# Routing tail of a hybrid layer: tiles 4 and 5 sorted as a pair, router work per column half

## Chip, cores and metric

The kernel runs on one core of a Trainium2 chip. The metric is the device time of one execution in microseconds (us). The engines are TensorE (PE; its weight loads PEld), VectorE (DVE), ScalarE (ACT), GpSimd (POOL) and the SyncE queue (SP), which only issues transfers. Each engine executes its instructions in the order in which they are written for it, and waits on semaphores for the others.

## Reference

A layer on 1024 latent tokens of width 1024 with 256 context tokens. Attention and a gated scan (DeltaNet) run side by side on one input projection; an output projection and a gated residual join them. A router then lets each of 16 experts choose its 128 strongest tokens.

```python
x = x + g1 * y_lat
h2 = modulate(rmsnorm(x, norm2_w[l]), sh2, sc2)
x = x + g2 * expert_choice_ffn(h2, router_w[l], w_gate[l], w_up[l], w_down[l])

# expert_choice_ffn
affinity = jax.nn.softmax((h @ router_w).astype(jnp.float32), axis=-1)
gates, idx = lax.top_k(jnp.swapaxes(affinity, 1, 2), cap)      # cap = 128
xg = jax.vmap(lambda hb, ib: hb[ib])(h, idx)
hid = jax.nn.silu(jnp.einsum('becd,edf->becf', xg, w_gate)) * jnp.einsum('becd,edf->becf', xg, w_up)
y = jnp.einsum('becf,efd->becd', hid, w_down) * gates[..., None].astype(h.dtype)
```

## The kernel before

Stages in order of time: adaLN vectors and the input projection (to about 411 us); the rest of the scan together with attention (to about 876 us, TensorE the busy engine); the output stage per token tile of 128 (eight tiles, tile 7 ends at about 957 us); the routing tail (to about 986 us); 16 experts (to the end).

The output stage has three functions per tile `t`. `out_norm(t)` normalizes the scan's output and builds the two operands `mh` and `ml`. `out_mm(t)` multiplies them with the output weights in two halves of 512 columns, 24 matmuls into `ps_d` each (lines 1283 to 1285), and VectorE adds the residual per half (`xres<-ps_d,xres`, line 1286). `out_route(t)` transposes the tile (line 1301), copies the transposes to `xT`, multiplies with the router weights `rwm` (line 1306, two groups of four), takes the sum of squares (`j<-xres`, line 1312), forms `logit`, its maximum `mx` and the softmax `aff`, and writes the normalized row `xn` for the later gather.

The top 128 of 1024 tokens per expert are found by sorting. `top_in(t)` brings the probabilities of a segment of tiles (dictionary `SEG`: tiles 0 to 3 as one, then each tile alone) on partitions, `top_out(t)` sorts lists with 8-wide maxima (`srt`, `at`), moves the sorted lists to the 16 experts' partitions by selection matmuls, and merges. For tiles 0 to 3 the selection matmuls are `ps_t<-srt` (line 1411) and ScalarE copies them to `lists` (lines 1416 and 1417); VectorE merges them as `m_3x`, `m_3y`. For a single tile four lists of 32 go through `ps_l` (line 1403) and `lists` (VectorE, line 1405) and are joined as `j2` and `j1`. Each result is merged into the running top list, named `t4` to `t7`; one merge step is a max and a min instruction of VectorE (`bitonic`, lines 1347 and 1348), 14 for a merge of 128. The last is `t7x`; `m` is its smallest value, the threshold of each expert, and `route()` makes slots, indices (`idx`) and gathers (`xg<-h,idx`) from it. Then the first expert matmul can start (`ps_m<-ehi,xx`, line 1612).

The order on each engine is set by a list scheduler from the program's order, priorities and modelled times. `tc.high_priority(-LP)` around a `top_out` puts its instructions behind others that are ready; the selection matmuls of single tiles are raised with `HP`.

`router_consts` (line 1182) makes the router's constants from the adaLN vectors in memory (`modrow`): column loads into `m2c`, `sh2` and `A2`, the modulated router weights `rwm`, and the bias `rbias` by a product with ones (`ps_d<-rwbs`, line 1207). In the prelude of attention (about 411 to 426 us) TensorE also transposes k (`ps_a<-consts,ksplit`, line 1057, 40 matmuls) and q (`ps_t<-consts,sr_sp`, line 1081), and VectorE finishes the last gate rows `zz` (line 626) and casts `kts` (line 1061).

## Time and profile before

| | |
|---|---|
| time, median of 3 runs | 1571.92 us (1571.24 to 1575.38) |
| profiled execution, its time | 1576.82 us |
| profiled execution, its span | 1575.1 us |
| TensorE busy | 1453.7 us (92%) |
| VectorE busy | 1175.2 us (75%) |
| ScalarE busy | 941.5 us (60%) |
| GpSimd busy | 252.2 us (16%) |
| chain that ended last, by engine | PE 63%, DVE 16%, DMA 10%, ACT 5% |

The span is the time from the first to the last recorded instruction of the profiled execution; what lies around it is 1.7 us. Rows of the trace give the start of an instruction, its duration, engine, line, output and inputs with shapes, and in brackets the idle time of its engine just before it with what ended it. Rows with xN put N adjacent instructions together. A view of stretches gives busy time of every engine, the granted TensorE clock as a share of full speed and the busy share of the transfer engines.

### The profile page before, as it was taken

The page shows a single profiled execution, that of the slowest core. Times are in us where ns is not written, and L with a number is a line of the kernel's source. Part 1 is how long each engine was busy: PE and PEld are TensorE (multiplying, and loading weights), DVE is VectorE, ACT ScalarE, POOL GpSimd, SP SyncE. Part 2 cuts the span into 40 slices and gives each one's busy share as a digit, 9 for nine tenths or more (in the row PEclk, how much of TensorE's full clock was granted, in tenths as well). Part 3 has the DMA queues.
Part 4 walks back from the last instruction along what each step waited for, and adds up shares of the span by engine and source line. Part 5 has one row for each costly group of instructions (what it writes and reads, how often), then busy time and mean ns, then how long its engine had stood idle before and what let it go on. Part 6 is the DMA issues. An engine that isn't in the chain of part 4 may idle for free.

```text
span 1575.1 us, 25623 instructions
## 1 busy us (share of the span) xinstructions
PE 1453.7 (92%) x9416; PEld 1177.5 (75%) x9416; DVE 1175.2 (75%) x2456; ACT 941.5 (60%) x1513; POOL 252.2 (16%) x230
## 2 busy tenths in 40 slices
PE   4999998987899998999899994999999999999996
PEld 1887787887778777887677663888888887777775
DVE  1824578698677686466666588899999998988886
ACT  1815454434376543556756442788887877777763
POOL 0000003323111112101400112011111211341001
PEclk7899999998999999899999997999999999999999
DMA  9356825777835456532333655889999999999991
GB/s 336 115 185 207 289 77 176 216 242 252 216 86 165 125 166 190 150 98 68 125 110 121 220 215 220 338 323 405 392 389 399 392 379 337 383 353 357 377 359 29
DMA packets 187049, 377.28 MB, mean 240 GB/s; under 512 B 47631, under 2 KB 124187, under 8 KB 159403
## 3 DMA queue, kind: packets, MB, share of 16 engines
q1 hardware_dynamic: 176320, 339.94, 61.3%
q0 software_dynamic: 7488, 29.36, 6.3%
q10 hardware_dynamic: 3115, 6.34, 1.0%
q8 instruction: 74, 1.21, 0.3%
q14 instruction: 52, 0.43, 0.1%
HBM read 321.91 MB, written 53.68 MB: 238 GB/s over the span
## 4 chain that ended last, share of the span: by engine, by line
PE 63%; DVE 16%; DMA 10%; ACT 5%; issue 3%; POOL 1%; SPq 1%; POOLq 0%; ACTq 0%; DVEq 0%
PE ps_m L1617 9%; PE ps_m L1612 8%; PE ps_m L1614 8%; PE ps_t L1130 4%; DVE elo L1599 4%; PE ps_a L1113 3%; PE ps_t L1123 3%; PE ps_s L442 3%; PE ps_s L444 3%; PE ps_s L443 3%; PE ps_d L976 1%; DMA woraw<-in_w_out 1%; PE ps_d L297 1%; PE ps_d L982 1%; PE ps_d L991 1%
## 5 line engine op out<-in xcount | busy, mean ns | idle before, releaser
L1599 DVE TENSOR_TENSOR elo<-eraw,ehi 128x2048 fp32r<-128x2048 f32 x102 | 229.2, 2285 | 16.1 <-ACT ehi L1588 16.0
L1588 ACT ACTIVATE ehi<-eraw 128x2048 fp32r<-128x2048 f32 x105 | 199.3, 1926 | 43.2 <-PE ps_m L1614 38.2
L1612 PE MATMUL ps_m<-ehi,xx 128*128 128x512 f32 x512 | 161.7, 397 | 2.2 <-ACT ehi L1588 2.2
L1614 PE MATMUL ps_m<-ehi,xx 128*128 128x512 f32 x512 | 159.5, 393 | 0.0
L1617 PE MATMUL ps_m<-elo,xx 128*128 128x512 f32 x512 | 139.6, 394 | 9.1 <-DVE elo L1599 8.9
L1116 DVE TENSOR_SCALAR_CACHE_REDUCE prob<-ps_a 128x416 f32<-128x416 f32 (+1 forms) x192 | 109.5, 596 | 26.5 <-PE ps_a L1113 16.3
L1599 DVE TENSOR_TENSOR elo<-fraw,ehi 128x2048 fp32r<-128x2048 f32 x51 | 115.6, 2287 | 12.4 <-ACT ehi L1588 12.3
L1617 PEld LDWEIGHTS ps_m<-elo,xx 128*128 128x128 f32 x512 | 94.7, 188 | 34.6 <-DVE elo L1599 15.8
L1674 POOL DMA_INDIRECT out_x<-ey,idx x16 | 70.9, 4430 | 291.0 <-DVE ey L1672 291.0
L1113 PE MATMUL ps_a<-kts,QT 128*128 128x416 f32 (+1 forms) x384 | 108.8, 389 | 4.2 <-DVE prob L1116 4.2
L1614 PEld LDWEIGHTS ps_m<-ehi,xx 128*128 128x128 f32 x512 | 96.4, 189 | 20.7 <-issue 0.2
L1612 PEld LDWEIGHTS ps_m<-ehi,xx 128*128 128x128 f32 x512 | 94.6, 189 | 22.7 <-ACT ehi L1588 4.1
L1124 ACT ACTIVATE PT<-ps_t 128x512 f32<-128x512 f32 (+1 forms) x192 | 93.5, 525 | 29.1 <-PE ps_t L1123 27.3
L1123 PE MATMUL ps_t<-consts,prob 128*128 128x128 f32 x640 | 100.8, 283 | 3.4 <-ACT PT L1124 1.7
L1588 ACT ACTIVATE ehi<-fraw 128x2048 fp32r<-128x2048 f32 x51 | 97.8, 1930 | 9.4 <-PE ps_m L1614 9.4
L434 PE MATMUL ps_s<-whi,hh 128*128 128x256 f32 (+1 forms) x336 | 98.8, 295 | 0.5 <-ACT zz L636 0.4
L1119 ACT ACTIVATE prob<-prob,mn 128x1280 f32<-128x1280 f32 x64 | 87.3, 1364 | 19.0 <-DVE mn L1118 18.3
L436 PE MATMUL ps_s<-whi,hl 128*128 128x256 f32 (+1 forms) x336 | 95.8, 289 | 0.2 <-DVE hl L411 0.2
L435 PE MATMUL ps_s<-wlo,hh 128*128 128x256 f32 (+1 forms) x336 | 95.9, 288 | 0.0
L442 PE MATMUL ps_s<-hh,whi 128*128 128x512 f32 (+1 forms) x256 | 95.5, 373 | 0.0
L444 PE MATMUL ps_s<-hh,wlo 128*128 128x512 f32 (+1 forms) x256 | 94.7, 370 | 0.0
L443 PE MATMUL ps_s<-hl,whi 128*128 128x512 f32 (+1 forms) x256 | 94.0, 367 | 0.0
(431 smaller groups left out, 3403.7 us busy)
## 6 DMA issues: line engine op xcount, KB each, us to landing
eraw<-in_w_up SPq DMA_DIRECT2D x38, 1024.0 KB, 8.1
eraw<-in_w_down SPq DMA_DIRECT2D x32, 1024.0 KB, 7.3
eraw<-in_w_gate SPq DMA_DIRECT2D x31, 1024.0 KB, 9.5
wmod<-in_w_mod SPq DMA_DIRECT2D x24, 1024.0 KB, 6.1
fraw<-in_w_down SPq DMA_DIRECT2D x21, 1024.0 KB, 7.0
fraw<-in_w_gate SPq DMA_DIRECT2D x16, 1024.0 KB, 8.0
fqraw<-in_w_gate SPq DMA_DIRECT2D x16, 1024.0 KB, 8.9
fraw<-in_w_up SPq DMA_DIRECT2D x14, 1024.0 KB, 8.4
```

Source lines behind the costliest of these rows:

```text
L434: self.nc.tensor.matmul(ps[:, :n], self.hh[:, k, ts], hi[:, k, a:a + n], start=st, stop=False)
L442: self.nc.tensor.matmul(ps[:, :n], hi[:, k, a:a + P], self.hh[:, k, ts], start=st, stop=False)
L443: self.nc.tensor.matmul(ps[:, :n], hi[:, k, a:a + P], self.hl[:, k, ts], start=False, stop=False)
L444: self.nc.tensor.matmul(ps[:, :n], lo[:, k, a:a + P], self.hh[:, k, ts], start=False, stop=en)
L1113: nc.tensor.matmul(ps[:, k0:min(k0 + 512, w)], QT[:, h, i], self.KTs[:, kv * 2 + x, ks], start=x == 0, stop=x == 1)
L1116: v.tensor_scalar(pr[:, c0:c0 + w], ps[:, :w], -1.0, 3e38, op0=ALU.mult, op1=ALU.min, accum_out=mn[:, y:y + 1])
L1123: nc.tensor.transpose(pt[:, x * P:(x + 1) * P], pr[:, (k0 + x) * P:(k0 + x + 1) * P], self.ident)
L1588: nc.scalar.activation(hi, raw, AF.Copy)
L1599: nc.vector.tensor_tensor(lo, raw, hi, op=ALU.subtract)
L1612: mm(banks[a], xh[:, q], hi[:, cs], start=q == 0, stop=False)
L1614: mm(banks[a], xl[:, q], hi[:, cs], start=False, stop=False)
L1617: mm(banks[a], xh[:, q], parts[q][1][:, cs], start=False, stop=q == KT - 1)
```

## The change

1. The segments become tiles 0 to 3, 4 and 5 together, 6, and 7. The pair has eight lists of 32, joined by `m2` and `jp` and a merge `m2`. `top_in(4)` and `top_out(4)` are gone. The buffers `lists3`, `m2x` and `m2y` are single and shared by tile 3's segment and the pair.
2. `out_route` transposes contiguous columns (the router weights are loaded to match, in 64-byte pieces) and takes the sum of squares per half of 512 columns, with two accumulators.
3. The copy of the row `xn` is issued after the softmax exponential.
4. `router_consts` loads the adaLN vectors for the router as 8 rows of 128 (`wraw`), adds them on 8 partitions, transposes twice on TensorE into `ps_d`, and multiplies the router weights from there. The columns for the experts (`sh2`, `A2`) stay.

```diff
@@ build @@
-        at4 = self.top_in(4)
...
-        with self.tc.high_priority(-LP):
-            self.top_out(4, at4)
@@ router_consts @@
+        mr = pool.tile([P, 4, 256], F32, name="wraw", tag="wraw", bufs=2)[:KT]
+        mr = mr.rearrange("p a b -> p (a b)")[:, :5 * P].rearrange("p (v c) -> p v c", v=5)
+        for i in range(2):
+            nc.sync.dma_start(mr[:, i], dram(self.modrow, (3 + i) * D, [[P, KT], [1, P]]))
+            nc.sync.dma_start(mr[:, 2 + i], dram(A["b_mod"], (3 + i) * D, [[P, KT], [1, P]]))
+        nc.sync.dma_start(mr[:, 4], dram(A["norm2_w"], 0, [[P, KT], [1, P]]))
...
+        pm = self.bank("d")
+        for i in range(2):
+            nc.tensor.transpose(pm[:, KT * i:KT * i + KT], mr[:, i], self.ident[:KT, :KT])
...
-        v.tensor_tensor(rb, rw, self.sh2[:, :, None].to_broadcast([P, KT, NE]), op=ALU.mult)
+        v.tensor_tensor(rb, rw, pm[:, :KT, None].to_broadcast([P, KT, NE]), op=ALU.mult)
...
-        v.tensor_tensor(self.rw[:, :, :NE], rw, self.A2[:, :, None].to_broadcast([P, KT, NE]), op=ALU.mult)
+        v.tensor_tensor(self.rw[:, :, :NE], rw, pm[:, KT:2 * KT, None].to_broadcast([P, KT, NE]), op=ALU.mult)
@@ out_route @@
-                nc.tensor.transpose(pt[:, i * P:(i + 1) * P], xv[:, 4 * g + i], self.ident)
+                nc.tensor.transpose(pt[:, i * P:(i + 1) * P], x1[:, (4 * g + i) * P:(4 * g + i + 1) * P], self.ident)
+
+            nc.scalar.activation(junk, x1[:, 512 * g:512 * g + 512], AF.Square, scale=D ** -0.5, accum_out=ss[:, g:g + 1])
...
-        nc.scalar.activation(junk, x1, AF.Square, accum_out=ss)
...
-        nc.scalar.activation(self.aff[:, t], lo, AF.Exp, bias=mx[:, 0:1], accum_out=mx[:, 1:2])
+        ex = nc.scalar.activation(self.aff[:, t], lo, AF.Exp, bias=mx[:, 0:1], accum_out=mx[:, 1:2])
...
-        nc.scalar.activation(xn, x1, AF.Copy, scale=r2)
+        with self.tc.issue_after(ex.ins):
+            nc.scalar.activation(xn, x1, AF.Copy, scale=r2)
@@ merge and top_out @@
-    SEG = {3: 0, 4: 4, 5: 5, 6: 6, 7: 7}
+    SEG = {3: 0, 5: 4, 6: 6, 7: 7}
...
+                for i in range(n):
+                    for g in range(4):
+                        c = 32 * g + NE * (2 - n + i)
+                        nc.tensor.matmul(ps[:, 4 * i + g], self.ident[:, c:c + NE], srt, start=True, stop=True)
+            L = self.os.tile([NE, P if n == 1 else 4 * P], F32, name="lists" if n == 1 else "lists3", bufs=3 - n)
...
+            if n == 1:
+                m = self.join(self.join(L, "j2"), "j1")
+            else:
+                m = self.join(self.join(L, "m2"), "jp")
+                m = self.merge(m[:, 0:1], m[:, 1:2], 1, "m2")
...
+            m = self.merge(L[:, 0::2], L[:, 1::2], 2, "m2")
```

**Tile 3's selection matmuls on TensorE.** First the kernel before, at the start of tile 6's routing: the last product of `out_mm(6)`, tile 7's scan transposes (`zl`), a selection matmul (`srt`), tile 6's transposes and the start of `out_mm(7)`.

```order
L1285 MATMUL ps_d<-wo1h,ml 128x512
L1263 MATMUL ps_d<-consts,zl 128x128 x4
L1411 MATMUL ps_t<-srt_10223,consts 16x128
L1301 MATMUL ps_t<-consts,xres 128x128 x8
L1283 MATMUL ps_d<-wo0h,mh 128x512
```

Now the changed kernel, at the end of the second half of `out_mm(7)`; behind it are tile 7's transposes.

```order
L1294 MATMUL ps_d<-wo1h,ml 128x512
L1429 MATMUL ps_t<-srt_10237,consts 16x128
L1292 MATMUL ps_d<-wo1h,mh 128x512
L1429 MATMUL ps_t<-srt_10237,consts 16x128
L1293 MATMUL ps_d<-wo1l,mh 128x512
L1294 MATMUL ps_d<-wo1h,ml 128x512
L1292 MATMUL ps_d<-wo1h,mh 128x512
L1293 MATMUL ps_d<-wo1l,mh 128x512
L1294 MATMUL ps_d<-wo1h,ml 128x512
L1311 MATMUL ps_t<-consts,xres 128x128 x8
```

The selection matmuls moved from the start of `out_mm(7)` to its end. ScalarE's copy of them (`lists<-ps_t 16x384`) moved with them, from ahead of tile 6's `lg` to behind tile 7's first Square.

**Tile 3's merge on VectorE.** The kernel before: its first step (`m_3x<-lists`) stands within tile 6's reciprocal root (`rs_a`, `rs_r`) and logits; tile 7's first `xres` follows 23 rows after it, the second 61.

```order
L132 TENSOR_TENSOR rs_a<-rs_a,rs_h 128x1
L133 SCALAR_TENSOR_TENSOR rs_r<-rs_a,rs_r 128x1
L1369 TENSOR_TENSOR m_3x<-lists_10259 16x256
L131 TENSOR_TENSOR rs_a<-rs_r 128x1
L1347 TENSOR_TENSOR m_3y<-m_3x 16x2x64
L132 TENSOR_TENSOR rs_a<-rs_a,rs_h 128x1
L1348 TENSOR_TENSOR m_3y<-m_3x 16x2x64
```

The changed kernel, from the last steps of tile 6's sort on; `xres` are tile 7's two residual additions, `lists_10565` on the last row but two is the pair's.

```order
L1295 TENSOR_TENSOR xres<-ps_d,xres 128x512
L1349 MATCH_REPLACE at_10542<-srt_10755,at_10542 128x32
L1347 MAX srt_10755<-at_10542 128x8
L1380 TENSOR_TENSOR m2x<-lists_10273 16x256
L1358 TENSOR_TENSOR m2y<-m2x 16x2x64
L1359 TENSOR_TENSOR m2y<-m2x 16x2x64
L1295 TENSOR_TENSOR xres<-ps_d,xres 128x512
L1358 TENSOR_TENSOR m2x<-m2y 16x4x32
L1359 TENSOR_TENSOR m2x<-m2y 16x4x32
L1419 COPY lists_10565<-ps_l 16x256
L1358 TENSOR_TENSOR m2y<-m2x 16x8x16
L1359 TENSOR_TENSOR m2y<-m2x 16x8x16
```

The first merge step on tile 3's lists moved behind tile 7's first residual addition, and all but three of its steps behind the second.

**The prelude of attention.** VectorE before, up to the scores' first reduction (`prob`):

```order
L626 SCALAR_TENSOR_TENSOR zz<-zt,ps_s 128x256 x2
L1209 COPY rbias<-ps_d 128x16
L626 SCALAR_TENSOR_TENSOR zz<-zt,ps_s 128x256
L1061 CAST kts<-ps_a 128x4x128 x5
L1116 TENSOR_SCALAR prob,mn<-ps_a 128x448
```

and in the changed kernel:

```order
L623 SCALAR_TENSOR_TENSOR zz<-zt,ps_s 128x256 x2
L1209 TENSOR_TENSOR rwb<-rw,ps_d 128x128
L1214 TENSOR_TENSOR rwm<-rw,ps_d 128x8x16
L623 SCALAR_TENSOR_TENSOR zz<-zt,ps_s 128x256
L1211 TENSOR_REDUCE rwbs<-rwb 128x16
L1218 COPY rbias<-ps_d 128x16
L1058 CAST kts<-ps_a 128x4x128 x5
```

The reduction `rwbs`, which was made at the start of the kernel, now stands behind the last `zz`. TensorE's `ps_d<-rwbs` still stands ahead of all k transposes, there with two new transposes of `wraw` ahead of it:

```order
L433 MATMUL ps_s<-whi,hl 128x256
L1205 MATMUL ps_d<-consts,wraw 128x8 x2
L1216 MATMUL ps_d<-rwbs,consts 128x16
L1054 MATMUL ps_a<-consts,ksplit 128x128 x32
L1078 MATMUL ps_t<-consts,sr_sp 128x128 x14
L1054 MATMUL ps_a<-consts,ksplit 128x128 x8
```

The row of 32 transposes follows `ps_d<-rwbs` in both kernels; what is new is what that product waits for.

## Rows read from the trace of the kernel before

**Rows 1.** Stretches: length, busy time by engine, clock, transfer share, GB/s.

```profile
414.00:417.00 3.00, 3.00 (x16) 2.96 (x14) 0.00 (x0) 1.08 (x3) 0.60 (x2) 0.50 1.04 349
426.00:600.00 174.00, 171.91 (x1738) 137.83 (x1736) 129.70 (x415) 103.01 (x220) 29.56 (x28) 1.00 0.50 141
918.00:942.00 24.00, 22.20 (x142) 16.52 (x143) 21.83 (x123) 7.29 (x21) 5.79 (x13) 1.00 0.41 169
942.00:957.00 15.00, 14.68 (x92) 10.49 (x90) 13.86 (x84) 5.28 (x11) 2.25 (x7) 1.00 0.18 71
976.00:978.00 2.00, 0.38 (x8) 0.29 (x8) 1.40 (x3) 0.00 (x0) 0.00 (x0) 0.50 0.03 12
1100.00:1200.00 100.00, 100.00 (x486) 83.19 (x485) 95.45 (x65) 81.02 (x71) 14.89 (x5) 1.00 1.01 390
```

**Rows 2.** Timeline of VectorE, 950 to 973 us: start, duration, what.

```profile
950.77 0.69 DVE L1286 TENSOR_TENSOR xres<-ps_d,xres 128x512 f32<-128x512 f32 x1
...
956.78 0.69 DVE L1286 TENSOR_TENSOR xres<-ps_d,xres 128x512 f32<-128x512 f32 x1
957.39 0.20 DVE L1347 TENSOR_TENSOR t4y<-t4x 16x64 f32<-16x64 f32 x1
957.52 0.21 DVE L1348 TENSOR_TENSOR t4y<-t4x 16x64 f32<-16x64 f32 x1
...
958.61 0.27 DVE L1369 TENSOR_TENSOR t5x<-t4y,j1x 16x128 f32<-16x128 f32 x1
958.81 0.13 DVE L1313 TENSOR_SCALAR ss<-ss 128x1 f32<-128x1 f32 x1
...
972.01 0.21 DVE L1348 TENSOR_TENSOR t6y<-t6x 16x64 f32<-16x64 f32 x1
972.25 0.28 DVE L1369 TENSOR_TENSOR t7x<-t6y,j1x 16x128 f32<-16x128 f32 x1
972.57 0.27 DVE L238 TENSOR_REDUCE m<-t7x 16x1 f32<-16x128 f32 x1
```

**Rows 3.** Timeline of TensorE after `m`.

```profile
972.90 0.60 PE L1453 MATMUL ps_m<-consts,m 16*128 16x16 f32 x2 [6.40 <-DVE m L238]
...
986.58 0.77 PE L1612 MATMUL ps_m<-ehi,xx 128*128 128x512 f32 x1
```

**Rows 4.** Timeline, tile 3's lists on TensorE, ScalarE and VectorE.

```profile
941.88 0.39 PE L1411 MATMUL ps_t<-srt,consts 64*16 64x128 f32 x2
...
945.09 0.46 ACT L1417 ACTIVATE lists<-ps_t 16x384 f32<-16x384 f32 x1
...
945.84 0.41 DVE L1369 TENSOR_TENSOR m_3x<-lists 16x256 f32<-16x256 f32 x1
```

**Rows 5.** Timeline of ScalarE and VectorE, tile 7's `out_route`.

```profile
957.56 1.06 ACT L1312 ACTIVATE j<-xres 128x1024 bf16<-128x1024 f32 x1 [9.18 <-issue]
...
958.61 1.07 ACT L1302 ACTIVATE xT<-ps_t 128x512 f32<-128x512 f32 x2
...
961.63 0.15 DVE L1320 TENSOR_REDUCE mx<-logit 128x1 f32<-128x16 f32 x1
...
962.33 0.29 ACT L1321 ACTIVATE aff<-logit,mx 128x16 f32<-128x16 f32 x1
```

**Rows 6.** Timeline of TensorE, a wait in the output stage.

```profile
918.52 0.27 PE L1385 MATMUL ps_t<-consts,aff 128*32 128x32 f32 x8 [1.53 <-DVE aff L1323]
```

**Rows 7.** Timelines of SyncE's queue, TensorE and VectorE ahead of attention.

```profile
358.69 0.53 SPq L806 DMA_DIRECT2D kq<-sqT  x1
...
413.68 3.56 PE L1057 MATMUL ps_a<-consts,ksplit 128*128 128x128 f32 x16 [2.42 <-DVE rbias L1209]
...
418.15 0.42 DVE L626 SCALAR_TENSOR_TENSOR zz<-zt,ps_s 128x256 f32<-128x256 f32 x1 [4.53 <-DMA sz<-zz]
...
419.23 1.53 PE L1057 MATMUL ps_a<-consts,ksplit 128*128 128x128 f32 x12 [0.77 <-DVE kts L1061]
...
425.59 2.60 PE L1113 MATMUL ps_a<-kts,QT 128*128 128x448 f32 x11
```

More of the change, by code (lines that the diff above doesn't have):

```diff
@@ L1296, in out_route @@
         xT = wo.tile([P, KT, P], F32, name="xT", bufs=1)
-        xv = x1.rearrange("p (q k) -> p k q", k=KT)
+        ss = wo.tile([P, 2], F32, name="ss2", bufs=2)
+        junk = wo.tile([P, 512], BF, name="j2", bufs=1)
         for g in range(2):
@@ L1309, in out_route @@
         nc.scalar.activation(lg, pl[:, :P], AF.Copy)
-        ss = wo.tile([P, 1], F32, name="ss2", bufs=2)
-        junk = wo.tile([P, D], BF, name="j2", bufs=1)
-        nc.scalar.activation(junk, x1, AF.Square, accum_out=ss)
-        v.tensor_scalar(ss, ss, 1.0 / D, EPS, op0=ALU.mult, op1=ALU.add)
-        r2 = self.rsqrt(wo, ss, 1, "n2")
+        ms = wo.tile([P, 1], F32, name="ms2", bufs=2)
+        v.tensor_scalar(ms, ss[:, 0:1], ss[:, 1:2], EPS, op0=ALU.add, op1=ALU.add)
+        r2 = self.rsqrt(wo, ms, 1, "n2")
         pl = self.bank("r" if "r" in self.tags else "d")
@@ L1356, in join @@
         _, n, s = L.shape
-        x = self.os.tile([NE, n // 2, 2 * s], F32, name=name + "x", bufs=2)
-        y = self.os.tile([NE, n // 2, 2 * s], F32, name=name + "y", bufs=2)
+        b = 2 if n * s == P else 1
+        x, y = (self.os.tile([NE, n * s], F32, name=name + i, bufs=b).rearrange("p (g s) -> p g s", s=2 * s) for i in "xy")
         a, b = L[:, 0::2], L[:, 1::2, ::-1]
@@ L1366, in merge @@
         v = self.nc.vector
-        x = self.os.tile([NE, G, P], F32, name=name + "x")
-        y = self.os.tile([NE, G, P], F32, name=name + "y")
+        w = 2 * P if name == "m2" else G * P
+        x, y = (self.os.tile([NE, w], F32, name=name + i)[:, :G * P].rearrange("p (g s) -> p g s", s=P) for i in "xy")
         v.tensor_tensor(x, a, b[:, :, ::-1], op=ALU.max)
         return self.bitonic(x, y, P) if sort else x
-    SEG = {3: 0, 4: 4, 5: 5, 6: 6, 7: 7}
+    SEG = {3: 0, 5: 4, 6: 6, 7: 7}
     def top_in(self, t):
@@ L1379, in top_in @@
         pa = self.bank("t")
-        if n == 1:
+        if n <= 2:
             at = self.os.tile([P, 32], F32, name=f"at{t}")
@@ L1398, in top_out @@
         srt = self.sort(at, f"srt{t}")
-        if n == 1:
-            ps = self.bank("l")[:NE, :P].rearrange("p (n q) -> p n q", n=4)
+        if n <= 2:
+            ps = self.bank("l")[:NE, :P * n].rearrange("p (n q) -> p n q", q=32)
             with self.tc.high_priority(HP):
-                for g in range(4):
-                    nc.tensor.matmul(ps[:, g], self.ident[:, 32 * g + NE:32 * g + 32], srt, start=True, stop=True)
-            L = self.os.tile([NE, 4, 32], F32, name="lists", bufs=2)
-            nc.vector.tensor_copy(L, ps)
-            m = self.join(self.join(L, "j2"), "j1")
+                for i in range(n):
[3 more added lines that the diff above has]
+            L = self.os.tile([NE, P if n == 1 else 4 * P], F32, name="lists" if n == 1 else "lists3", bufs=3 - n)
+            L = L[:, :n * P].rearrange("p (n q) -> p n q", q=32)
+            nc.vector.tensor_copy(L, ps)
+            if n == 1:
[3 more added lines that the diff above has]
+                m = self.merge(m[:, 0:1], m[:, 1:2], 1, "m2")
         else:
```

16 lines of the change are left out of this document (7 added, 9 removed).

## Prediction

> **What bounds the kernel now.** I began with the table of stages [rows 1]. In the attention stretch 426 to 600 us TensorE is busy 171.91 of 174 us, in the experts 100.00 of 100; between the two lies the output stage, and behind that a hole in which TensorE waits for the routing. The chain of waits shows why: it leaves TensorE with the last residual addition of tile 7 (956.78), follows VectorE through sort and merges to `m` (972.57) and comes back to TensorE at 972.90 [rows 2, 3]; the first expert matmul starts at 986.58 [rows 3]. So whatever happens ahead of `m` on VectorE after 956.78 moves the experts. It moves them one for one: the weights for the experts are prefetched into a fixed set of buffers, and at 976 to 978 the transfers have fallen to a share of 0.03 [rows 1], so the buffers are full before the experts begin; a later start brings in no further bytes, and the experts that follow have TensorE at 100%.
>
> The stretch 956.78 to 972.57 is 15.79 us of VectorE in its own written order, 112 instructions (the residual addition and `m` included). 81 of them are merge steps on 64 elements, 3 on 128. Full of independent work VectorE starts a 64-element step every 0.13 to 0.135 us (957.39 to 957.52) and needs 0.20 from a 128-element step to the next (958.61 to 958.81); a step that waits for the one just ahead starts after 0.24 (972.01 to 972.25) [rows 2].
>
> **The change, the tail.** Its intent is fewer, wider steps for tiles 4 and 5. What decides is where they stand, and the order shows that. In the kernel before, tile 3's selection matmuls run at 941.88, ahead of tile 6's transposes, ScalarE copies the lists at 945.09, and VectorE's first merge on them is at 945.84 [rows 4]. That is five microseconds ahead of the first half of tile 7's residual addition (950.77) and eleven ahead of the second (956.78) [rows 2]; in those eleven VectorE finishes tile 3, does most of tile 4 and begins tile 5 while TensorE still multiplies. In the changed kernel the last two of these selection matmuls stand near the end of the second half of `out_mm(7)`, two groups of three matmuls before its end, and ScalarE's copy stands behind the Square of tile 7's first half. VectorE's first merge on the lists, `m2x<-lists` on 256 elements, comes after tile 7's first residual addition, and only two more steps stand ahead of the second one. VectorE works in order: it will stand idle for about 4 us before 956, and all the rest of tile 3, the whole pair, tile 6 and tile 7 comes after the second residual addition.
>
> Counted in the order from that addition to `m`: 180 instructions in place of 112. 108 are on 64 elements (27 more), 43 on 128 (40 more); there is one list copy of 128 elements more and one of 256; sort, rsqrt and softmax keep their counts. By the spacings, 27 x 0.135 = 3.6, 40 x 0.20 = 8.0, and for the copies 0.20 + 0.3 (a 256-element step lasts 0.41 [rows 4], so 0.3 to 0.41) = 0.5. Tile 6's last seven pairs now stand alone between `t6x` and `t7x`, where before tile 7's join lay between them: 0.24 + 0.135 instead of 2 x 0.135, 7 x 0.105 = 0.7. Sum **+12.8 us**, on a stretch that VectorE alone bounds. If all steps overlapped as well as the 64-element ones, it is 68 x 0.135 + 0.3 = 9.5; if the 40 wide ones stood in pairs alone, it is some 2 more. 12.8 is kept, since three chains are interleaved there until the last.
>
> Here a rule can be weighed. The Trainium skill, "VectorE: DVE Perf Modes", section "The DRAIN you can't avoid", says that a following operation begins when the pipe of the one before is empty, with an exception for operations that nothing holds. By the full rule an estimate from the durations (0.20 for 64 elements, 0.27 for 128, [rows 2]) would be 27 x 0.20 + 40 x 0.27 + 0.7 = 16.9 us instead of 12.8; the starts 0.13 apart of steps that last 0.20 show that the exception rules here, and I keep the spacing.
>
> The savings that were meant: the Square of 1024 columns took 1.06 and stood ahead of the transposed copies, two in 1.07 [rows 5]; half of it can run while TensorE makes the second half, so 0.5 less. The Exp waited behind the 1.15 us row copy until 962.33, though its maximum was there at 961.63 + 0.15 [rows 5]: 0.5 less. Both shorten the way to tile 7's probabilities. In the changed kernel VectorE has the merges of tile 3, the pair and tile 6 to do meanwhile and never runs dry, so the 1.0 us is worth nothing. Taking contiguous instead of strided columns in the transposes costs and gains nothing that a row shows: TensorE's part is hidden behind the same VectorE queue. The row copy's store moves behind the expert preparations on GpSimd's queue and is needed by the gather, which begins only after `m` and what follows it; hidden.
>
> **The output stage** itself could shift the residual addition at 956.78. TensorE lacks 1.80 us of 24 in 918 to 942 and 0.32 of 15 in 942 to 957 [rows 1]; its wait of 1.53 us for the probabilities of the tile ahead, which ends at 918.52 [rows 6], lies two thirds (1.0) ahead of that stretch. If the change removed all of it: -3.1 us. Against that, VectorE's part of `out_norm(6)` now has more of tile 3's sort ahead of it, and the selection for tile 6 waits between the router's two matmul groups of tile 7 for VectorE's copy of the pair's lists; I put +2 on it, about one such wait. I take 0.
>
> **The prelude of attention.** The router's constants are now made by TensorE and VectorE where before they were ready long ahead. Before, TensorE made the bias product and went on at 413.68 with the k transposes [rows 7]. Now the product needs `rwbs`, and that reduction stands on VectorE behind the last `zz`, which waits 4.53 us for a store and runs at 418.15 for 0.42. TensorE therefore stands until 418.57 + some 0.6 (an estimate: the reduction at the 0.27 of a 128-element step [rows 2], and as much again for the way to TensorE) = 419.2, that is 5.5 us. Behind it are 32 + 14 + 8 = 54 transposes before the scores, at 1.53 / 12 = 0.128 each: 6.9, so the scores would start at 426.1 instead of 425.59, +0.5. After the idle time before 413.68 the clock stood at 0.50 from 414 to 417, and 16 transposes took 3.56 instead of 2.05 [rows 1, 7]; the longer idle time will have the same behind it, +1.5; the casts add a few tenths. Lower end 0.5, upper end 5.5 (the whole wait stays); I take **+2.3**, near the lower end, since the waits of before in 417 to 425 are for transfers that have then landed. TensorE is full after that, so it counts. The five row loads queue on SP behind a load at 358.69 [rows 7] with over 50 us in hand; 0 in the sum, and inside the upper end otherwise. Router weights in 64-byte pieces are loaded among the first transfers of all and needed only here: 0.
>
> **The rest.** The scheduler also reshuffles scan and attention on all engines. TensorE is at 171.91 of 174 us there [rows 1], so a gain is about 2 us at most per such stretch and a loss has no such bound; I take 0 and 4 us on either side.
>
> **Sum.** 12.8 + 2.3 + 0 + 0 = +15.1. On the profiled execution, 1576.82, that is 1591.9; this execution lay 4.9 above the median 1571.92, so on the median 1587.0.
>
> **Rivals.**
> A, milder: output stage 3.1 earlier, prelude 0.5, merges 9.5 to 12.8: 9.5 + 0.5 - 3.1 = +7 to 12.8 + 0.5 - 3.1 = +10, 1579 to 1582. For it: fewer VectorE steps at 919 to 944. Against: TensorE's few waits there. Chance 0.20.
> B, harder: the prelude's 5.5 in full and 4 from the reshuffle: 12.8 + 5.5 + 4 = +22, 1594. Chance 0.13.
> C, faster: the pair does what fewer steps promise. If tile 3's lists reached VectorE before tile 7's first residual addition, the merges would lie under `out_mm(7)` as before; the 1.0 us of the Square and the Exp would count, and up to 2 us of steps fewer in the tail: -1 to -3, so 1569 to 1571. It decides at one place: whether VectorE's first merge on tile 3's lists starts before 951. The order speaks against it, and only an order on the chip other than the written one could bring it. Chance 0.05. The Trainium skill's "VectorE: DVE Perf Modes", section "Rules for kernel authors", advises to minimize the number of operations; the rows agree on the price (0.20 for a step twice as wide against 0.27 for two), and by that rule alone C would be the result.
> D, no difference: the tail is 12.8 later but the experts absorb it, because a transfer, not TensorE, sets their pace: then +2.3 or less, 1572 to 1574. Against it: the share of 0.03 at 976 to 978 and TensorE's 100.00 of 100 [rows 1]. Chance 0.06.
> E, the change doesn't do what it says: the pair, now on single buffers shared with tile 3, waits for tile 3's merge step by step and VectorE is left with lone pairs: 12.8 + 2.3 + 0.105 x 20 = +17, 1589. It would look like the forecast. Chance 0.08.
>
> **How the numbers follow.** The forecast has 0.48, with 1582 to 1591 for itself; A 0.20, B 0.13, E 0.08, C 0.05, D 0.06. A measurement of this kernel tells 0.3% (4.7 us) from no change. Slower by more: forecast, A, B and E, 0.89. Within it: D and part of C, 0.08. Faster: the rest of C, 0.03. Range 1577 to 1595: from A with 2 us of the reshuffle to B.
>
> **What would show it.** Right: `m2x<-lists` at 955 to 956.5 with VectorE idle ahead of it; the second residual addition within 2 us of 956.8; `m` some 28 us behind it instead of 15.8; TensorE's wait for `m` near 19 us instead of 6.40; TensorE idle at 411 to 419 with VectorE's `rbias` as the releaser. Wrong: merges of the pair ahead of the second residual addition, a distance to `m` below 20 us, or an expert phase that is shorter than before.

## The result and the profile after

The changed kernel takes 1595.83 us (median of 4 runs, 1591.62 to 1598.41), the kernel before 1572.43 us; the ratio is 1.014, with a 95% interval of 1.0122 to 1.0158, so 19 to 25 us slower. The profiled execution took 1595.43 us, its span is 1593.7 us, 18.6 more than the span before.

VectorE at the end of the routing, timeline of the changed kernel, columns as in [rows 2]; `lists` in the second row is tile 3's, `xres` tile 7's second residual addition:

```profile
956.63 0.20 DVE L1347 MAX8 srt<-at 128x8 f32<-128x32 f32 x1
961.36 0.41 DVE L1380 TENSOR_TENSOR m2x<-lists 16x256 f32<-16x256 f32 x1 [4.54 <-ACT lists L1432]
961.80 0.28 DVE L1358 TENSOR_TENSOR m2y<-m2x 16x128 f32<-16x128 f32 x1
962.01 0.27 DVE L1359 TENSOR_TENSOR m2y<-m2x 16x128 f32<-16x128 f32 x1
962.21 0.69 DVE L1295 TENSOR_TENSOR xres<-ps_d,xres 128x512 f32<-128x512 f32 x1
...
963.55 0.27 DVE L1358 TENSOR_TENSOR m2y<-m2x 16x128 f32<-16x128 f32 x1
963.75 0.27 DVE L1359 TENSOR_TENSOR m2y<-m2x 16x128 f32<-16x128 f32 x1
...
990.40 0.28 DVE L1380 TENSOR_TENSOR t7x<-t6y,j1x 16x128 f32<-16x128 f32 x1
990.71 0.27 DVE L235 TENSOR_REDUCE m<-t7x 16x1 f32<-16x128 f32 x1
```

These rows answer to [rows 2]. VectorE stood idle for 4.54 us until ScalarE had copied tile 3's lists, then had three merge steps ahead of the residual addition and everything else behind it. From that addition to `m` it takes 990.71 - 962.21 = 28.50 us; it was 15.79. Steps on 128 elements start 0.20 apart and last 0.27, as in [rows 2].

ScalarE and TensorE in the same stretch:

```profile
960.85 0.48 ACT L1432 ACTIVATE lists<-ps_t 16x384 f32<-16x384 f32 x1 [3.61 <-PE ps_t L1429]
...
971.00 0.31 ACT L1331 ACTIVATE aff<-logit,mx 128x16 f32<-128x16 f32 x1 [5.78 <-DVE mx L1330]
...
972.02 0.33 PE L1396 MATMUL ps_t<-consts,aff 128*32 128x32 f32 x8 [6.35 <-DVE aff L1333]
974.88 0.59 PE L1416 MATMUL ps_l<-srt,consts 128*16 128x32 f32 x8 [2.52 <-DVE srt L1347]
991.04 0.60 PE L1468 MATMUL ps_m<-consts,m 16*128 16x16 f32 x2 [15.58 <-DVE m L235]
```

Two of these waits of TensorE in the kernel before; the third, for `m`, is in [rows 3]:

```profile
963.39 0.33 PE L1385 MATMUL ps_t<-consts,aff 128*32 128x32 f32 x8 [2.38 <-DVE aff L1323]
965.91 0.58 PE L1403 MATMUL ps_l<-srt,consts 128*16 128x32 f32 x8 [2.18 <-DVE j1x L1348]
```

The copy of tile 3's lists is at 960.85; it was at 945.09 [rows 4]. Tile 7's own probabilities are late too: ScalarE's Exp waits 5.78 us for VectorE's maximum, and TensorE waits 6.35 us for `aff`, before 2.38. Its wait for tile 7's sorted lists is 2.52 us (2.18), the one for `m` 15.58 (6.40): 4.0, 0.3 and 9.2 us more.

Stretches of the changed kernel, columns as in [rows 1]:

```profile
942.00:962.00 20.00, 20.00 (x112) 14.64 (x111) 6.94 (x33) 5.89 (x15) 2.23 (x7) 1.00 0.15 62
962.00:991.00 29.00, 3.57 (x51) 2.42 (x49) 28.53 (x186) 8.92 (x11) 2.35 (x7) 0.61 0.64 254
984.00:988.00 4.00, 0.00 (x0) 0.00 (x0) 3.86 (x27) 0.00 (x0) 0.00 (x0) 0.50 0.00 0
1100.00:1200.00 100.00, 100.00 (x486) 83.18 (x485) 94.32 (x68) 82.57 (x77) 17.27 (x6) 1.00 1.01 390
```

In 942 to 962 TensorE is full and VectorE does 6.94 us of 20; in the stretch of 29 us behind it VectorE does 28.53 and TensorE 3.57. At 984 to 988 nothing is transferred, and the experts run at 100% of TensorE as before.

The prelude of attention on TensorE in the changed kernel, and the last two rows on VectorE that it waits for:

```profile
411.91 0.29 PE L1205 MATMUL ps_d<-consts,wraw 8*128 8x8 f32 x2
418.94 0.58 PE L1216 MATMUL ps_d<-rwbs,consts 128*128 128x16 f32 x2 [6.74 <-DVE rwbs L1211]
419.36 5.17 PE L1054 MATMUL ps_a<-consts,ksplit 128*128 128x128 f32 x32
...
427.82 0.84 PE L1110 MATMUL ps_a<-kts,QT 128*128 128x448 f32 x3
```

```profile
418.09 0.42 DVE L623 SCALAR_TENSOR_TENSOR zz<-zt,ps_s 128x256 f32<-128x256 f32 x1 [2.39 <-DMA sz<-zz]
418.43 0.36 DVE L1211 TENSOR_REDUCE rwbs<-rwb 128x16 f32<-128x128 f32 x1
```

These answer to [rows 7]. The product waits 6.74 us for `rwbs`, which follows the last `zz`; the scores start at 427.82, before at 425.59.

### The profile page after: what moved, and what is told of

Read it like the earlier page. It is cut to its first block, busy times and chain, and to the rows that moved or that the text cites. A ratio compares the mean times of both kernels' runs of the same rounds, so it can differ in the third digit from the quotient of the medians.

```text
span 1593.7 us, 25595 instructions
## 1 busy us (share of the span) xinstructions
PE 1455.4 (91%) x9410; PEld 1179.8 (74%) x9410; DVE 1178.2 (74%) x2420; ACT 943.5 (59%) x1529; POOL 252.4 (16%) x230
## 4 chain that ended last, share of the span: by engine, by line
PE 61%; DVE 17%; DMA 12%; ACT 5%; issue 3%; POOL 1%; SPq 1%; POOLq 0%; DVEq 0%; ACTq 0%
PE ps_m L1632 8%; PE ps_m L1627 8%; PE ps_m L1629 8%; DVE elo L1614 4%; PE ps_t L1127 4%; PE ps_t L1120 3%; PE ps_a L1110 3%; PE ps_s L439 3%; PE ps_s L441 3%; PE ps_s L440 3%; PE ps_d L973 1%; DMA of<-so 1%; DMA woraw<-in_w_out 1%; PE ps_d L294 1%; PE ps_d L979 1%
## 5 line engine op out<-in xcount | busy, mean ns | idle before, releaser
L1632 PEld LDWEIGHTS ps_m<-elo,xx 128*128 128x128 f32 x512 | 94.9, 189 | 34.6 <-DVE elo L1614 15.8
L1116 ACT ACTIVATE prob<-prob,mn 128x1280 f32<-128x1280 f32 x64 | 87.2, 1363 | 15.3 <-DVE mn L1115 14.7
```

What stands on the lines that cost most here:

```text
L1632: mm(banks[a], xh[:, q], parts[q][1][:, cs], start=False, stop=q == KT - 1)
```

## Where the time is: stages of every trace

The stages below are worked out from the starts of instructions in each trace. "Projection" is the time to the end of the input projection (start of the last `ps_s` matmul plus its 0.28 us); "prelude" from there to the first scores (`ps_a<-kts,QT`); "attention" from there to the first `xres`; "output" to tile 7's second `xres`; "tail" to `m`; "route" to the first expert matmul (`ps_m<-ehi`); "experts" to the end of the span. The names of the runs are explained in the next section.

| kernel | projection | prelude | attention | output | tail | route | experts |
|---|---|---|---|---|---|---|---|
| before | 411.1 | 14.4 | 382.8 | 148.4 | 15.8 | 14.0 | 588.5 |
| before, again (e8) | 409.0 | 12.0 | 381.6 | 152.1 | 15.8 | 13.7 | 587.8 |
| after | 412.0 | 15.8 | 384.7 | 149.7 | 28.5 | 14.3 | 588.7 |
| after, again (e11) | 411.8 | 15.3 | 384.0 | 149.4 | 28.4 | 13.8 | 587.9 |
| e1 | 411.0 | 15.6 | 386.3 | 148.8 | 14.9 | 14.2 | 588.4 |
| e2 | 412.0 | 13.9 | 385.9 | 146.7 | 28.5 | 14.3 | 588.7 |
| e3 | 412.9 | 15.2 | 384.4 | 147.3 | 14.9 | 14.4 | 588.4 |
| e4 | 408.6 | 12.2 | 382.9 | 149.8 | 14.7 | 15.4 | 590.1 |
| e5 | 409.8 | 15.8 | 382.6 | 152.2 | 22.4 | 14.9 | 588.6 |
| e6 | 409.5 | 12.0 | 382.2 | 152.0 | 14.7 | 14.7 | 590.3 |
| e7 | 413.1 | 10.2 | 387.1 | 146.8 | 14.9 | 14.4 | 588.0 |
| e9 | 413.0 | 9.6 | 382.5 | 150.8 | 14.7 | 14.1 | 588.4 |
| e10 | 410.1 | 12.7 | 382.6 | 149.9 | 14.6 | 14.5 | 589.8 |

The tail is the same within 0.07 us in every execution of an order (15.79 twice; 28.50, 28.43 and 28.50). The stages ahead of it vary by up to 3.7 us from one execution of the same kernel to the next (the output stage of the kernel before, 148.4 and 152.1), and the single times show it: the runs of the kernel before lie between 1565.79 and 1583.71 us in all. A tail is therefore read from one trace, the rest only from several.

## The experiments

A ratio is to runs of the kernel before made beside the experiment: their medians are 1573.69 us for e1 to e4, 1573.66 for e5 to e8 and 1574.57 for e9 to e11. The interval behind it is the 95% interval.

**e1: tile 3's selection raised.** One line of priority in the changed kernel:

```diff
+            with self.tc.high_priority(HP):
-            for i in range(1, n):
-                nc.tensor.matmul(ps[:NE, i], ...)
+                for i in range(1, n):
+                    nc.tensor.matmul(ps[:NE, i], ...)
```

> The changed kernel, with tile 3's selection matmuls raised in priority as those of the other tiles are; nothing else. They now stand ahead of tile 5's and tile 6's work on TensorE, and 90 instructions are left on VectorE between tile 7's second residual addition and m (60 merge steps on 64 elements, 3 on 128), where the changed kernel has 180 and the kernel before 112. Theory (the late lists alone make the tail long): that distance goes from 28.5 us to 15.8 - 21 x 0.135 = 13 us, TensorE's first expert matmul comes 15 us earlier than in the changed kernel, and the time is about 1595.8 - 15 = 1581 us. Rival (the wide steps of the pair on single shared buffers are slow themselves): the distance stays above 20 us and the time above 1588 us.

Measured: 1581.24 us (10 runs), ratio to before 1.0052 (1.003 to 1.0073). VectorE:

```profile
927.22 0.41 DVE L1380 TENSOR_TENSOR m2x<-lists 16x256 f32<-16x256 f32 x1
...
961.75 0.69 DVE L1295 TENSOR_TENSOR xres<-ps_d,xres 128x512 f32<-128x512 f32 x1
...
976.64 0.27 DVE L235 TENSOR_REDUCE m<-t7x 16x1 f32<-16x128 f32 x1
```

The first merge on tile 3's lists is at 927.22, and from the second residual addition to `m` it takes 14.89 us with the same pair, the same single buffers and the same wide steps. Of the 28.50 us, 13.6 were the order alone; the rival falls. That it is 14.9 and not 13 says that VectorE's count no longer sets the tail; e6 shows what does.

**e2: the bias product later.** The product and its copy leave `router_consts` and go to `out_open`; `rwbs` is kept in a tile that lives that long.

```diff
-        pb = self.bank("d")
-        nc.tensor.matmul(pb[:, :NE], self.one, rwb, start=True, stop=True)
-        self.rbias = k.tile([P, NE], F32, name="rbias")
-        v.tensor_copy(self.rbias, pb[:, :NE])
...
     def out_open(self):
+        pb = self.bank("d")
+        nc.tensor.matmul(pb[:, :NE], self.one, self.rwb, start=True, stop=True)
+        self.rbias = k.tile([P, NE], F32, name="rbias")
+        nc.vector.tensor_copy(self.rbias, pb[:, :NE])
```

> The changed kernel, with the router's bias product and its copy moved from the prelude of attention to the place where the output stage opens; nothing else. Theory (TensorE's wait for rwbs delays the scores by 2.2 us): the k transposes start near 413 us instead of 419.4, the scores near 425.5 instead of 427.8, everything behind comes about 2 us earlier, the time is about 1593.5 us; the tail keeps its 28.5 us. Rival (the wait stands in the place of others, for the stores of the gate rows and the k rows): the scores stay within 0.7 us of 427.8 and the time within 1 us of 1595.8. Second rival (the whole distance of 5.5 us in the output stage comes from the prelude): 1590 us.

Measured: 1589.37 us (4 runs), ratio 1.010 (1.0061 to 1.014). TensorE:

```profile
411.89 0.29 PE L1205 MATMUL ps_d<-consts,wraw 8*128 8x8 f32 x2
414.42 2.87 PE L1054 MATMUL ps_a<-consts,ksplit 128*128 128x128 f32 x16 [2.24 <-DVE rwm L1214]
...
425.90 1.44 PE L1110 MATMUL ps_a<-kts,QT 128*128 128x448 f32 x5
```

The scores start at 425.90, near the theory's 425.5, and the prelude is 13.9 us. TensorE no longer waits for `rwbs`, but for `rwm`: 2.24 us, ended by VectorE's multiplication that reads the constants from `ps_d`. The code gives the k transposes no use of the constants; their PSUM belongs to the next stage's pool, though, which takes over the banks of the pool that `ps_d` belongs to, and that is the tie I see. So the product was one of two ties to VectorE, and moving it alone leaves the prelude 1.4 to 1.9 us shorter than in the two traces of the changed kernel. The tail keeps its 28.50. The time is the 1590 us of the second rival, but not by its mechanism: in the trace the last residual addition comes 3.7 us earlier (958.47 against 962.21) and not 5.5. The 6.5 us below the changed kernel are more than these terms; the intervals of the two ratios overlap.

**e3: both.** The edits of e1 and e2.

> The changed kernel with both edits, the raised selection matmuls and the late bias product. Theory (two independent delays): 15 + 2 us below the changed kernel, 1579 us, still above the kernel before by what the scan and attention lost in their own order (about 3 us) and more, though the tail is shorter than before. Rival (the tail's lateness and the prelude are all there is): 1570 us or less, below the kernel before.

Measured: 1577.80 us (10 runs), ratio 1.0029 (1.0007 to 1.0052). The tail is 14.88, the prelude 15.2 (in this execution TensorE waited 3.69 us for `rwm`). The time is near the theory's 1579 us, but the trace doesn't show that the second delay is gone: e1's prelude is 15.6. 4 us remain against the kernel before although the tail is 0.9 shorter. In the traces they lie in projection and prelude, 3.9 and 3.2 us more than in e8; attention's 2.8 more is less than the 4.8 by which the output stage is shorter.

**e4: constants and columns as before.** `router_consts` and the transposes' columns from the kernel before, everything else of the change.

```diff
-        pm = self.bank("d")
...
+        v.tensor_tensor(rb, rw, self.sh2[:, :, None].to_broadcast([P, KT, NE]), op=ALU.mult)
...
-                nc.tensor.transpose(pt[:, i * P:(i + 1) * P], x1[:, (4 * g + i) * P:(4 * g + i + 1) * P], self.ident)
+                nc.tensor.transpose(pt[:, i * P:(i + 1) * P], xv[:, 4 * g + i], self.ident)
```

> The changed kernel with the router's constants and the transposes' columns as in the kernel before (column loads, strided columns); the pair, the Square per half and the Exp ahead of the row copy stay. In its order tile 3's selection matmuls stand ahead of tile 6's work again, and 87 instructions stand on VectorE between tile 7's second residual addition and m. Theory (the pair itself costs nothing, the lateness of tile 3's lists and the prelude came with the constants' new place in the modelled times): the distance is 13 us, the scores start near 425.6, and the time is 3 to 4 us below the kernel before, 1569 us. Rival (the pair is what lengthens the tail): distance above 20 us, time above 1580 us.

Measured: 1574.44 us (10 runs), ratio 1.0004 (0.9983 to 1.0025). VectorE:

```profile
926.38 0.41 DVE L1369 TENSOR_TENSOR m2x<-lists 16x256 f32<-16x256 f32 x1
...
953.49 0.69 DVE L1283 TENSOR_TENSOR xres<-ps_d,xres 128x512 f32<-128x512 f32 x1
...
962.55 0.28 DVE L1408 COPY lists<-ps_l 16x128 f32<-16x128 f32 x1 [0.64 <-PE ps_l L1405]
...
968.16 0.27 DVE L235 TENSOR_REDUCE m<-t7x 16x1 f32<-16x128 f32 x1
```

With the pair, tile 3's merge starts at 926.38 and the tail is 14.67 us. The pair doesn't lengthen it; the rival falls. Prelude, projection and attention are those of the kernel before; the scores start at 420.9, as in e8, and not at the 425.6 of the first trace. The 3 to 4 us of gain did not come. The tail gave 1.1 and not 2.8, since tile 7's chain bounds it (e6), and in this trace route and experts, 15.4 and 590.1 us, take more than that back (14.0 and 588.5 in the first trace of the kernel before, 13.7 and 587.8 in e8). 1.1 us (0.07%) cannot be told from no change here.

**e5: constants and columns alone.** The counterpart, in the kernel before: the whole hunk of `router_consts`, and

```diff
-        xv = x1.rearrange("p (q k) -> p k q", k=KT)
...
-                nc.tensor.transpose(pt[:, i * P:(i + 1) * P], xv[:, 4 * g + i], self.ident)
+                nc.tensor.transpose(pt[:, i * P:(i + 1) * P], x1[:, (4 * g + i) * P:(4 * g + i + 1) * P], self.ident)
```

> The kernel before, with the router's constants by rows and the contiguous columns in the transposes (parts 4 and the first half of 2) and nothing else: no pair, one Square of 1024, the Exp behind the row copy. Tile 3's selection matmuls stand at the end of out_mm(7) in this order too, and VectorE has 143 instructions between tile 7's second residual addition and m (96 merge steps on 64 elements, 20 on 128). Theory (the constants' place moves the lists late, the pair only makes the steps behind wider): distance 15.8 + 15 x 0.135 + 17 x 0.20 = 21 us, and prelude and attention as in the changed kernel: 1573.7 + 5.5 + 4 to 6 = 1583 to 1585 us. Rival (the pair moves them): distance 16 us, time near 1576 us.

Measured: 1586.39 us (4 runs), ratio 1.0089 (1.0056 to 1.0123). VectorE:

```profile
960.00 0.41 DVE L1380 TENSOR_TENSOR m_3x<-lists 16x256 f32<-16x256 f32 x1 [1.51 <-ACT lists L1428]
960.38 0.69 DVE L1298 TENSOR_TENSOR xres<-ps_d,xres 128x512 f32<-128x512 f32 x1
...
982.75 0.28 DVE L238 TENSOR_REDUCE m<-t7x 16x1 f32<-16x128 f32 x1
```

Without the pair, tile 3's first merge is again just ahead of the last residual addition, and the tail is 22.37 us (21 expected). So this part of the change made the lists late. The rest of it, above all the pair with its wide steps, made the queue behind them 6.1 us longer: 12 more on 64 elements and 24 more on 128, counted in the two traces, are 12 x 0.135 + 24 x 0.20 = 6.4 us by the spacings. The prelude is 15.8 us, as in the changed kernel (TensorE waited 6.20 us for `rwbs`), so this part brings that too. Attention, 382.6, is that of the kernel before, where the theory had the changed kernel's; the time is 1.4 us above its range. e1 says that the lateness was a matter of priority; e4 and e5 say which part brought it. Whether the constants or the columns of the transposes did it was not separated, and why the scheduler's modelled times turn the order there wasn't looked into: the order is what the runs share.

**e6: Square per half and Exp ahead alone,** in the kernel before, with strided columns.

```diff
+            nc.scalar.activation(junk, x1[:, 512 * g:512 * g + 512], AF.Square, scale=D ** -0.5, accum_out=ss[:, g:g + 1])
...
-        nc.scalar.activation(junk, x1, AF.Square, accum_out=ss)
...
+        with self.tc.issue_after(ex.ins):
+            nc.scalar.activation(xn, x1, AF.Copy, scale=r2)
```

> The kernel before, with only the Square per half and the Exp ahead of the row copy. 82 instructions on VectorE between tile 7's second residual addition and m. Theory (these two take 1.0 us off tile 7's own chain, which ends last once the lists are early): distance 14.7 us instead of 15.8, the time about 1 us below the kernel before, 1572.5 us, too little to be told from it. Rival (the merges, 30 instructions fewer, are the bound): distance 12 us, the time 4 us below.

Measured: 1574.55 us (10 runs), ratio 1.0008 (0.9987 to 1.0029). VectorE, then ScalarE:

```profile
955.74 0.69 DVE L1286 TENSOR_TENSOR xres<-ps_d,xres 128x512 f32<-128x512 f32 x1
...
964.80 0.28 DVE L1408 COPY lists<-ps_l 16x128 f32<-16x128 f32 x1 [0.77 <-PE ps_l L1406]
...
970.41 0.27 DVE L238 TENSOR_REDUCE m<-t7x 16x1 f32<-16x128 f32 x1
...
956.52 0.63 ACT L1305 ACTIVATE j<-xres 128x512 bf16<-128x512 f32 x1 [5.37 <-DVE xres L1286]
...
960.63 0.31 ACT L1323 ACTIVATE aff<-logit,mx 128x16 f32<-128x16 f32 x1 [1.50 <-DVE mx L1322]
...
960.94 1.13 ACT L1328 ACTIVATE xn<-xres,rs_r 128x1024 f32<-128x1024 f32 x1
```

The tail is 14.67 us, 1.1 less than before. Square and Exp do what they were meant to: the row copy stands behind the Exp, and TensorE gets tile 7's probabilities 5.9 us behind the addition (961.65) instead of 6.6 (963.39 - 956.78). That is 0.7 of the 1.1. The other 0.4 comes behind the copy of tile 7's lists on VectorE (964.80): from there to `m` it takes 5.61 us here and 5.61 in e4, with steps of tile 7 alone; before it took 6.04 (from 966.53), with steps of tile 6 among them. So here it is tile 7's chain that ends last.

The tail is the same as in e4 to the hundredth, with 57 merge steps on 64 elements in e4 and 52 here: with or without the pair, the number of steps isn't the bound. The Trainium skill, "VectorE: DVE Perf Modes", section "Rules for kernel authors", advises to minimize the number of operations in a chain. Here the trace shows the limit of that: the profile has 2456 records of VectorE in e6 and 2418 in e4, and the tail is 14.67 us in both, since the steps of the other tiles fit into the waits of tile 7's chain.

**e7: selection and constants early.** e1, with the whole block from the additions on `wraw` to the copy of `rbias` raised in priority.

```diff
+        with self.tc.high_priority(HP):
-        v.tensor_tensor(mr[:, 0:2], mr[:, 0:2], mr[:, 2:4], op=ALU.add)
+            v.tensor_tensor(mr[:, 0:2], mr[:, 0:2], mr[:, 2:4], op=ALU.add)
...
```

> The changed kernel with tile 3's selection matmuls raised, and the router's constants raised in the same way, so that TensorE's two transposes, VectorE's multiplications and the bias product stand within the input projection and not behind it. Theory (in the run with the bias late, TensorE's k transposes waited for rwm, VectorE's last reader of the PSUM bank of the constants, as long as for the product): with all of it early they follow the input projection within 1 us, and the scores start 12 to 13 us behind its end (15.8 in the changed kernel, 14.5 before, where the bias is waited for); the time is 2 to 3 us below the first of these runs, 1578.5 us. Rival (the transfers of the k rows set the scores): 14 us or more behind the projection's end, the time 1581 us.

Measured: 1580.01 us (8 runs), ratio 1.0049 (1.0028 to 1.007). TensorE:

```profile
412.99 1.91 PE L1054 MATMUL ps_a<-consts,ksplit 128*128 128x128 f32 x16
416.86 1.94 PE L1054 MATMUL ps_a<-consts,ksplit 128*128 128x128 f32 x16 [1.97 <-DMA ksplit<-sks]
...
423.35 1.93 PE L1110 MATMUL ps_a<-kts,QT 128*128 128x448 f32 x8
```

The k transposes follow the projection at once, and the scores start 10.2 us behind its end. So the two ties to VectorE are the prelude's delay (15.6 us in e1). But the median is only 1.2 us below e1's, between theory and rival. In the traces this projection ends 2.1 us later than e1's, attention is 0.8 longer (387.1 us, the longest of all) and the output stage 2.0 shorter, and the span is 4.7 us shorter; but the traced execution was the fastest of the 8 (1576.34 to 1583.03 us). How much of the prelude's 5.4 us lasts to the end is open.

**e8: the kernel before, again,** without an edit.

> The kernel before, unchanged, for a second trace. It tells how far the places of the scores and of the output stage vary from one execution to the next: if the distance from the scores to tile 7's second residual addition is again 531.2 us within 0.7, the 3.2 us that the changed kernel has more there are its own; if it varies by 2 us or more, they are not told apart from that.

Measured: 1573.70 us (one run). TensorE, and VectorE's last `zz`:

```profile
408.81 0.29 PE L1207 MATMUL ps_d<-rwbs,consts 128*128 128x16 f32 x2
412.25 5.38 PE L1057 MATMUL ps_a<-consts,ksplit 128*128 128x128 f32 x32 [3.15 <-DVE rbias L1209]
...
420.95 3.48 PE L1113 MATMUL ps_a<-kts,QT 128*128 128x448 f32 x15
...
414.06 0.42 DVE L626 SCALAR_TENSOR_TENSOR zz<-zt,ps_s 128x256 f32<-128x256 f32 x1 [1.87 <-DMA sz<-zz]
```

In this execution the last `zz` runs at 414.06 and the scores start at 420.95; in the first trace it waited for its store until 418.15, and the scores started at 425.59 [rows 7], 4.6 us later: 2.2 in the projection's end, 2.5 in the prelude. From the scores to tile 7's second residual addition it is 533.8 us against 531.2: 2.6 us between two executions of one kernel, so by what was laid down beforehand the changed kernel's 3.2 us more there cannot be told apart from chance. Attention alone is taken up at e11.

**e9: Square, Exp, and the bias early,** in the kernel before, to see whether a version beats both: e6, with the reduction `rwbs`, the product and its copy raised in priority.

```diff
+        with self.tc.high_priority(HP):
+            v.tensor_reduce(rwb, rb.rearrange("p k e -> p e k"), axis=AX.X, op=ALU.add)
...
+        with self.tc.high_priority(HP):
+            nc.tensor.matmul(pb[:, :NE], self.one, rwb, start=True, stop=True)
+            v.tensor_copy(self.rbias, pb[:, :NE])
```

> The kernel before with the Square per half, the Exp ahead of the row copy, and the bias product raised in priority, so that it and its copy stand within the input projection. Theory: TensorE's k transposes follow the projection's last matmul within 1 us (3.15 us behind it in the second trace of before, waiting for rbias), the scores start some 10 us behind its end instead of 12, the tail keeps 14.7 us instead of 15.8: 2 to 3 us below the kernel before, about 1571 us. Rival (what is won in the prelude is waited for again in attention, as in the run with constants and selection early, where attention took 387 us instead of 385): the distance from the scores to the first residual addition grows by 2 us, and the time is that of the kernel before within 1 us.

Measured: 1573.64 us (12 runs) against 1574.57 for the kernel before, ratio 0.9983 (0.9962 to 1.0005). TensorE:

```profile
412.88 1.91 PE L1057 MATMUL ps_a<-consts,ksplit 128*128 128x128 f32 x16
415.22 0.63 PE L1057 MATMUL ps_a<-consts,ksplit 128*128 128x128 f32 x4 [0.42 <-DMA ksplit<-sks]
...
422.61 1.63 PE L1113 MATMUL ps_a<-kts,QT 128*128 128x448 f32 x6
```

The transposes follow the projection at once and the prelude is 9.6 us, but the projection itself ends at 413.0: the scores start at 422.6, not earlier than the 420.9 to 421.6 of e4, e6 and e8. The time is the rival's, that of the kernel before within 1 us, but in this trace it is not attention that waits, as the rival had it (382.5 us): the projection ends later. The tail keeps its 14.66. The interval contains 1.

**e10: the pair with the bias early.** e4, with the priorities of e9.

> The changed kernel with the router's constants and the strided columns of the kernel before, and the bias product raised as in the other run of this call: pair, Square per half and Exp ahead stay. Theory: as the other run, since tile 7's own chain bounds the tail with the pair and without it (14.7 us): 1571 to 1572 us, the pair adding nothing. Rival (the pair's fewer steps free VectorE in the output stage): the stretch from tile 3's to tile 7's residual addition is 1 to 2 us shorter than in the other run, and the time 1 to 2 us lower.

Measured: 1573.65 us (12 runs), ratio 0.9981 (0.9961 to 1.0001). The tail is 14.64 and the time the same as in e9. The stretch that the rival names, from tile 3's to tile 7's second residual addition, is 68.6 us against 70.1 in e9, shorter by what it said; but the two traces of the kernel before have 70.4 and 73.9 there, so one pair of traces can't show it, and the time has nothing of it. The scores start at 422.8 us as in e9 (422.6), though the projection ends at 410.1 here: TensorE waits 1.78 us for the transfer of k rows. The pair adds nothing that can be measured. Neither e9 nor e10 can be told from the kernel before; both are some 22 us faster than the changed kernel.

**e11: the changed kernel, again,** without an edit.

> The changed kernel, unchanged, for a second trace. If the input projection ends at 411 to 413 us again (408.6 to 411.1 in the kernels with the constants of before) and attention takes 384 to 387 us from the scores to the first residual addition (381.7 to 382.9), these two belong to the changed order of scan and attention; the tail is 28.5 us and the first expert matmul 14.3 us behind m in any case.

Measured: 1592.29 us (one run). Projection 411.8, prelude 15.3, attention 384.0 and tail 28.43 are as expected, the route is 13.75 and not 14.3. The kernels that have the pair and the new constants together (after twice, e1, e2, e3, e7) take 384.0 to 387.1 us for attention; the others (before twice, e4, e5, e6, e9, e10) take 381.6 to 382.9. The ranges don't meet: in the changed order attention is 2 to 4 us longer. But its output stage is shorter, 146.7 to 149.7 us against 148.4 to 152.2. Both together are 531.7 to 535.1 us (mean 533.5) in the first group and 531.2 to 534.8 (mean 533.2) in the second, so the traces show no loss there in all. The projection's end doesn't separate the groups: 411.0 to 413.1 against 408.6 to 413.0 (e9).

## Why the prediction was right, and where it was off

The direction and the main mechanism were right, the size was too small: 1587.0 forecast, 1595.8 measured, 0.8 above the upper end of the range; the interval of the ratio, on 1572.43, begins at 1591.6. The forecast stood on 3 runs of the kernel before; over the 69 runs of all comparisons their median is 1573.96, and the difference is 21.9 us where +15.1 was forecast.

**The tail, +12.8: right.** 28.50 - 15.79 = 12.71 in the first pair of traces, 28.43 - 15.79 = 12.64 in the second. VectorE's idle time of about 4 us was 4.54. The spacing of 0.135 and 0.20 carried the sum. The Trainium skill, "VectorE: DVE Perf Modes", "The DRAIN you can't avoid", taken without its exception, made an estimate of 16.9 us; the trace has 12.7 and decides for the spacing. Off was TensorE's wait for `m`: 19 us forecast, 15.58 measured, because tile 7's probabilities were late as well and the wait for them took 4.0 of the rest.

Off too were two of the places that were to show it. `m2x<-lists` came at 961.36 and the second residual addition at 962.21 (959.68 and 960.54 in the second trace), where 955 to 956.5 and 956.8 within 2 us had been named: what lies ahead of the tail had grown by 5.4 us in the first pair of traces and by 5.8 in the second.

**One for one into the experts: right.** Experts 588.5 and 588.7 us, the share of transfers 0.00 at 984 to 988; rival D falls. "The meant 1.0 us is worth nothing here" is right too. Where the lists are early (e4, e6) the tail is 1.1 us shorter than before, 0.7 of it ahead of tile 7's probabilities.

**The output stage, 0: right within its bounds.** 148.4 and 152.1 us before, 149.7 and 149.4 after.

**The prelude, +2.3: the mechanism right, the size mis-sized.** The bias product waited for `rwbs`, that for the last `zz`, and the k transposes followed at 419.36, forecast 419.2. e5 and e7 show that this is the delay: 15.8 us of prelude with the new constants and columns alone, 10.2 with them early. The term for the clock was 1.5 us; the 32 transposes took 5.17, 1.1 more than at 0.128 each (granted clock 0.50 in 418 to 421, 0.77 in 421 to 424).

The scores moved from 425.59 to 427.82, +2.2, but that agreement is luck. The step that failed is the row that the sum started from: in that one trace the last `zz` waited 4.53 us for its store. In e8, e4 and e6, with the same constants, VectorE's wait there is 1.87 to 2.48 us and the scores start at 420.9 to 421.6. The changed kernel's last `zz` runs at 418.09, where the forecast took it over from that row, but after a wait of 2.39 us. Against the second trace (420.95) the second one of the changed kernel (427.13) is 6.2 later: 2.9 in the projection's end, 3.3 in the prelude. The upper end of 5.5 that I had for it was nearer than the value taken. Whether the projection's 2.9 belongs to the change isn't shown.

**The rest, 0: right as a sum, not stage by stage.** Attention is 2 to 4 us longer in the changed order, and the output stage shorter by about as much (e11). The sum of the second pair of traces, which is free of the long wait for the store: projection +2.9, prelude +3.3, attention +2.4, output -2.7, tail +12.6, route 0.0, experts +0.1: 18.6, the difference of the spans, 1590.6 - 1572.0. The first pair gives 18.6 as well, with +2.2 to the scores and +3.2 in attention and output stage together. The medians of the result are 23.4 us apart, 4.8 more than either pair of traces, and 21.9 with all runs of the kernel before; with the variation from run to run of several us that stays open.

**Why the lists came late: not in the prediction.** It read the lateness off the order and ascribed it to no part. e4 and e5 show that the pair isn't the cause and that the router's constants and the columns of the transposes, together, are.

Still open: which of these two turns the order, which instructions of the changed order make attention longer and the output stage shorter, and why the projection ends where it does. No run changed that order alone.

## What to carry to other kernels

Where a scheduler sets the order, a change in one place can move a low-priority step far away; look in the new order for what is now behind the last thing on the critical engine, count it and price it with the spacing of starts, not with durations. An engine that idles just ahead of its longest queue is the sign, and one raised priority on the step that feeds it (e1) gave back 13.6 us of the tail. A row that waits for a transfer is no base for a difference until a second trace of the same kernel shows it again. A stage that grew is no loss until its neighbour has been looked at: attention's 2 to 4 us came back in the output stage.

## What the runs showed of the hardware

The same kernel's prelude took 14.4 us in one execution and 12.0 in another. In the longer one VectorE waited 4.53 us for the store of the last gate rows, in the other 1.87; TensorE's waits for the transfers of k and q rows were longer there too (0.59, 0.59 and 0.89 us against one of 0.20). VectorE's 112 or 180 instructions of the tail took the same time within 0.07 us in every trace (15.79 and 15.79; 28.50, 28.43, 28.50). Steps on 64 and 128 elements that last 0.20 and 0.27 us start 0.135 and 0.20 apart where nothing makes them wait for the one ahead, and 0.24 apart where it does (64 elements, [rows 2]); by these spacings 67 more of them and two more copies were forecast at 12.8 us, and the tail grew by 12.7.

A matmul into PSUM waited 2.24 us in e2 and 3.69 in e3 for a VectorE instruction that reads another tile of PSUM, `ps_d`, a tie that appears in no data dependence of the program and was not in the forecast; that it comes from the pool's handover is read from the code, and no run tried it apart.
